# Two residual blocks in float32: the end of a layer and the start of the next, done by halves of the tokens

## The chip, the cores and the metric

The kernel runs on one core of one Trainium2 chip. The metric is the time on the device in microseconds (us), as the median of several runs; less is better. The timed runs before took 2711.64, 2714.61 and 2717.73 us.

## The reference, cut to what matters

The program computes two blocks of a network for 512 tokens of 1024 features. The first block has four layers, each of which ends in the same way, and the change touches these four ends and nothing else:

```
x = x + rms_norm(retention(rms_norm(x, g)), g_post)            # layer 1
x = x + rms_norm(conv_ffn(rms_norm(x, g)), g_post)             # layer 2
x = x + rms_norm(diff_attention(rms_norm(x, g), kv), g_post)   # layer 3
x = x + rms_norm(conv_ffn(rms_norm(x, g)), g_post)             # layer 4

def rms_norm(x, g):
    return x * rsqrt(mean(x * x over the 1024 features) + 1e-6) * g
```

The second block (a convolution layer, a sparse attention and two feed-forward layers) has no norm on a layer's output. So a layer of the first block can add nothing to `x` before the sum of the squares of all 1024 output features of a token is known, and the next layer can start nothing before `x` is there.

## The kernel before, in words

Data lies with features on the 128 partitions and tokens along the free dimension, so `x` is eight tiles of 128 features by 512 tokens (`KD` is 8, `S` is 512). A float32 product is carried by three float32r passes (`mm3`, lines 202 to 204): both operands are kept as a high and a low part, made by ScalarE (high) and VectorE (low) in `pair` (lines 213 to 217).

Weights are a stream of 128x128 tiles in chunks of eight (`Stream`). SyncE loads chunks into four raw buffers; ScalarE writes the high part (line 106) and VectorE the low part (line 107) into one of three split buffers. A chunk is split as soon as TensorE is done with the chunk three before it. While `lo_engine` is set, line 107 runs on GpSimd in VectorE's place.

A *column* is one output tile of 128 features: a bank of PSUM that collects all its products (`col`). Each finished column of a layer's output is added to the layer's sum `hs`, squared on ScalarE (line 228) and added to `post`, the running sum of squares (line 229).

The *end of a layer* is `col_halves` (line 369): the last column alone, whose last products run first for tokens 0 to 255 and then for 256 to 511, both into one bank. After each half `done` (line 282) adds it to `hs` and squares it into a tile of its own. `last_out` also sets `lo_engine` to GpSimd, and `group` takes it back after its last step.

The *start of the next* is `group` (line 326) with an update: four columns at once in a feed-forward layer (`first = 2`: two pairs of gate and value), six in the attention and in the convolution layer. The contraction is outermost: for each of the eight tiles k of `x`, `Prep.step` makes the new `x` and its two parts, and `outer` issues for every column the two products with the high part (lines 353, 354), then the one with the low part (line 357). Tile 0 goes by halves of the tokens, the others whole.

The *norm between them* sits in `residual` (line 532), at tile 0 of the group. For each half of the tokens: sums over the partitions by small matmuls (`colsum`, line 238), square root on ScalarE (line 254), a Newton step on VectorE (lines 255 and 245 to 248), and a transpose on TensorE that spreads the result over the partitions (`spread`, line 261). The update of a tile is then a product (line 549) and a product with a sum (line 550) on VectorE, and `pair` follows (lines 216, 217), then the squares for the next norm (lines 225 to 229). Sums of both halves share one bank, spread values another.

Order: the program is written in Python, and a scheduler of the framework orders the instructions of each engine by their place in the program and a model of when they become ready. The place in the trace is therefore not always that in the code. Dependencies on PSUM are kept by bank.

Below, a *seam* is such an end of a layer with the start of the next: seam 1 follows the retention, seam 2 the first feed-forward layer, seam 3 the differential attention, seam 4 the second feed-forward layer.

## Time and profile before

| | |
|---|---|
| median of three timed runs | 2714.61 us (2711.64 to 2717.73) |
| span of the profiled execution | 2714.0 us |
| TensorE busy | 2670.7 us, 98% of the span |
| VectorE busy | 1687.1 us, 62% |
| ScalarE busy | 1192.5 us, 44% |
| GpSimd busy | 174.2 us, 6% |

The page of the profile gives the span from the first to the last instruction of one execution. No time of its own is given for that execution beside its span; the span lies 0.6 us under the median of the timed runs, which themselves lie 6 us apart. Busy times are shares of the whole program; a stretch is looked at by the view of windows, which gives for any piece of the span the busy time of each engine and the clock that TensorE was granted (1.00 is 2.4 GHz, 0.50 is 1.2 GHz). Matmuls are pipelined, so the duration shown for one is longer than the distance to the next: what a matmul costs is the distance of starts.

### The profile page before, as it was taken

The numbers are of one execution on the slowest core, as the hardware profiler recorded it, in microseconds if no ns is written. First come the engines' busy times: TensorE is split into PE (matmuls) and PEld (weight loads), VectorE is DVE, ScalarE is ACT, GpSimd is POOL, SyncE is SP. The second block draws the span as 40 slices with busy tenths as digits, with TensorE's granted clock in tenths as the row PEclk, the third lists the DMA queues.
The fourth block names the chain that finished last, engine by engine and source line by source line (L and its number), as shares of the span: only waits on it lengthen the run. The fifth ranks groups of instructions, "written<-read, shape, count | busy, mean of one in ns | idle before, by whom it ended". The sixth has DMA issues, their size and how long they took to land.

```text
span 2714.0 us, 34980 instructions
## 1 busy us (share of the span) xinstructions
PE 2670.7 (98%) x13875; PEld 2217.3 (82%) x13875; DVE 1687.1 (62%) x2695; ACT 1192.5 (44%) x1936; POOL 174.2 (6%) x147
## 2 busy tenths in 40 slices
PE   9999999999999999999999999999999999999999
PEld 8888887888888877888887578888888777888887
DVE  6545558736657687755748965545547788564453
ACT  5443434434445664533434244323337676442331
POOL 0000001000012101000005300000001111000000
PEclk9999999999999999999999989999999999999999
DMA  5223222332322112232323412223343101222222
GB/s 180 81 76 101 83 74 70 101 100 94 103 78 93 55 45 73 87 100 94 103 93 101 118 62 95 100 94 118 113 141 128 36 13 39 72 98 96 96 98 86
DMA packets 73252, 243.42 MB, mean 90 GB/s; under 512 B 9216, under 2 KB 12160, under 8 KB 73088
## 3 DMA queue, kind: packets, MB, share of 16 engines
q1 hardware_dynamic: 73088, 241.18, 26.9%
q8 instruction: 109, 1.79, 0.3%
q14 instruction: 55, 0.45, 0.1%
HBM read 229.63 MB, written 4.19 MB: 86 GB/s over the span
## 4 chain that ended last, share of the span: by engine, by line
PE 88%; DVE 8%; ACT 2%; issue 1%; POOL 1%; SPq 1%; DMA 0%; POOLq 0%; ACTq 0%; DVEq 0%
PE bank L202 24%; PE bank L204 24%; PE bank L203 24%; PE bank L353 3%; PE bank L357 3%; PE bank L354 3%; DVE bank L1000 2%; PE bank L691 2%; PE bank L747 1%; PE bank L1480 1%; DVE arena_f L550 1%; PE bank L238 1%; PE bank L886 1%; DVE w_spl L107 0%; DVE arena_r L217 0%
## 5 line engine op out<-in xcount | busy, mean ns | idle before, releaser
L202 PE MATMUL bank<-arena_r,w_spl 128*128 128x512 f32 (+1 forms) x2712 | 1061.8, 392 | 3.3 <-DVE arena_f L1050 1.9
L203 PE MATMUL bank<-arena_r,w_spl 128*128 128x512 f32 (+1 forms) x2712 | 1054.5, 389 | 0.7 <-DVE arena_r L214 0.7
L204 PE MATMUL bank<-arena_r,w_spl 128*128 128x512 f32 (+1 forms) x2712 | 1051.9, 388 | 0.0
L106 ACT ACTIVATE w_spl<-w_raw 128x1024 fp32r<-128x1024 f32 (+1 forms) x424 | 448.4, 1058 | 715.8 <-PE bank L203 471.6
L107 DVE TENSOR_TENSOR w_spl<-w_raw,w_spl 128x1024 fp32r<-128x1024 f32 (+1 forms) x392 | 480.5, 1226 | 387.0 <-ACT w_spl L106 384.1
L202 PEld LDWEIGHTS bank<-arena_r,w_spl 128*128 128x128 f32 x2712 | 509.8, 188 | 108.5 <-issue 4.1
L204 PEld LDWEIGHTS bank<-arena_r,w_spl 128*128 128x128 f32 x2712 | 509.5, 188 | 105.4 <-issue 1.6
L203 PEld LDWEIGHTS bank<-arena_r,w_spl 128*128 128x128 f32 x2712 | 509.8, 188 | 101.0 <-issue 1.4
L563 DVE SCALAR_TENSOR_TENSOR arena_f<-arena_f,vec 128x510 f32<-128x510 f32 (+1 forms) x264 | 195.7, 747 | 5.5 <-ACT arena_f L561 1.8
L213 ACT ACTIVATE arena_r<-arena_f 128x512 fp32r<-128x512 f32 (+1 forms) x153 | 91.9, 610 | 191.5 <-DVE arena_f L591 153.7
L353 PE MATMUL bank<-arena_r,w_spl 128*128 128x512 f32 (+1 forms) x410 | 162.9, 399 | 10.2 <-ACT arena_r L216 8.2
L354 PE MATMUL bank<-arena_r,w_spl 128*128 128x512 f32 (+1 forms) x410 | 160.5, 393 | 0.0
L586 DVE TENSOR_TENSOR arena_f<-bank,arena_f 128x512 f32<-128x512 f32 x88 | 60.7, 689 | 131.6 <-PE bank L204 131.6
L202 PE MATMUL bank<-w_spl,arena_r 128*128 128x256 f32 (+1 forms) x480 | 138.9, 290 | 2.1 <-ACT arena_r L1267 1.6
L204 PE MATMUL bank<-w_spl,arena_r 128*128 128x256 f32 (+1 forms) x480 | 136.7, 286 | 0.1
L203 PE MATMUL bank<-w_spl,arena_r 128*128 128x256 f32 (+1 forms) x480 | 136.4, 284 | 0.0
L214 DVE TENSOR_TENSOR arena_r<-arena_f,arena_r 128x512 fp32r<-128x512 f32 (+1 forms) x153 | 100.5, 670 | 38.3 <-ACT arena_r L213 37.5
L711 ACT ACTIVATE arena_f<-bank,small 128x128 f32<-128x128 f32 (+3 forms) x192 | 99.6, 525 | 50.2 <-DVE small L708 47.0
L107 POOL TENSOR_TENSOR w_spl<-w_raw,w_spl 128x1024 fp32r<-128x1024 f32 x32 | 79.6, 2489 | 616.8 <-ACT w_spl L106 612.2
L588 ACT ACTIVATE arena_f<-arena_f 128x512 f32<-128x512 f32 x88 | 55.5, 631 | 138.7 <-DVE arena_f L563 138.6
L561 ACT ACTIVATE arena_f<-arena_f,vec 128x512 f32<-128x512 f32 x132 | 106.2, 809 | 22.5 <-DVE arena_f L582 21.5
L582 DVE TENSOR_TENSOR arena_f<-bank,arena_f 128x512 f32<-128x512 f32 x88 | 60.5, 688 | 80.3 <-PE bank L204 71.9
(225 smaller groups left out, 2928.0 us busy)
## 6 DMA issues: line engine op xcount, KB each, us to landing
w_raw<-w SPq DMA_DIRECT2D x422, 512.0 KB, 3.4
arena_f<-tab SPq DMA_DIRECT2D x10, 256.0 KB, 3.5
arena_f<-x SPq DMA_DIRECT2D x8, 256.0 KB, 7.5
x_wait<-arena_f SPq DMA_DIRECT2D x8, 256.0 KB, 2.3
arena_f<-x_wait SPq DMA_DIRECT2D x8, 256.0 KB, 2.6
out<-arena_f SPq DMA_DIRECT2D x8, 256.0 KB, 2.2
arena_r<-arena_f SPq DMA_DIRECT2D x20, 64.0 KB, 2.0
arena_r<-arena_f SPq DMA_DIRECT2D x20, 63.9 KB, 2.0
```

The source lines that it names most:

```text
L106: self.nc.scalar.activation(hi, r, AF.Copy)
L107: (self.lo_engine or self.nc.vector).tensor_tensor(lo, r, hi, op=ALU.subtract)
L202: mm(out, a[0], b[0], start=start, stop=False, skip_group_check=skip)
L203: mm(out, a[0], b[1], start=False, stop=False, skip_group_check=skip)
L204: mm(out, a[1], b[0], start=False, stop=stop, skip_group_check=skip)
L213: self.nc.scalar.activation(h, src, AF.Copy)
L214: self.nc.vector.tensor_tensor(l, src, h, op=ALU.subtract)
L353: mm(b, w[0], hi[:, sl], start=(k == 0 and sl.start == 0), stop=False, skip_group_check=True)
L354: mm(b, w[1], hi[:, sl], start=False, stop=False, skip_group_check=True)
L561: nc.scalar.activation(c.a, u.a, AF.Identity, bias=self.v(cb, j), scale=self.v(cw, 2 * nj + j))
L563: nc.vector.scalar_tensor_tensor(c.a[:, d:], u.a[:, :S - d], self.v(cw, (2 - d) * nj + j), c.a[:, d:], op0=ALU.mult, op1=ALU.add)
L711: nc.scalar.activation(p.a[:, :n], outs[c], AF.Exp, bias=mx[:, c:c + 1], accum_out=sm[:, c:c + 1])
```

## The change

The last column of a layer's output was done by halves; now the last four columns are in the retention and the attention (16 weight tiles), and the last two in the feed-forward layers (22 weight tiles). All of them run for tokens 0 to 255 first, then all for 256 to 511, each half of each column in a bank of its own (`tail`). The sums and the norm of the first half are issued inside the second half. The order on TensorE within `tail`, and within the first three tiles of the next group, is fixed as written (`in_order`). The next group does its first three tiles of `x` for the first half of the tokens, then for the second (`group_halves`); sums and spread of the second half are issued after tiles 0 and 1 of the first. Since each weight tile is used in both passes, the stream is held: no chunk is split over one that the second pass still needs (`hold`). The feed-forward layers now start with six columns instead of four (`first = 3`). The low part of the weights is always made by VectorE. Squares of tiles 0 to 2 are made later, two to a step. In the diff, comments and early exits that are also gone are left out.

```diff
@@ class Stream, take
         if o == 0:
+            h = c if self.held is None else self.held
+            assert c < h + NSPL
             self.load(c + NRAW)
-            self.parts(c + NSPL)
+            self.parts(h + NSPL)
...
+    def hold(self, chunk=None):
+        self.held = chunk
+        self.parts(((len(self.order) - 1) // CHUNK if chunk is None else chunk) + NSPL)
@@ class Prep
-    def halves(self, k):
-        return HALVES if self.update is not None and k < 1 else (slice(0, S),)
+    def half(self, k, sl):
+        b = self.b
+        if len(self.xs) == k:
+            self.xs.append((b.R.get(), b.R.get()))
+        self.update.apply(k, sl)
+        b.pair(b.x[k].a[:, sl], b.v(self.g, k), [s.a[:, sl] for s in self.xs[k]])
+        if sl.stop == S and self.want:
+            self.squares.append(k)
...
+class Residual:
+    def sums(self, i):
+        b = self.bank[i] = self.b.P.get()
+        self.b.colsum(b, self.accs, 256, True, range(2 * i, 2 * i + 2))
+    def scale(self, i):
+        self.rs[i] = self.b.rstd(self.bank[i].a[:, 256:258], 2, D)
+    def spread(self, i):
+        self.b.spread(self.bank[i], self.rs[i], 0, 2)
+    def apply(self, k, sl):
+        b, nc = self.b, self.b.nc
+        for i, half in enumerate(HALVES):
+            if half.start < sl.start or half.stop > sl.stop:
+                continue
+            h = self.hs[k].a[:, half]
+            nc.vector.tensor_tensor(h, h, self.bank[i].a[:, 0:256], op=ALU.mult)
+        x = b.x[k].a[:, sl]
+        nc.vector.scalar_tensor_tensor(x, self.hs[k].a[:, sl], b.v(self.g, k), x, op0=ALU.mult, op1=ALU.add)
...
@@ class Build, in place of last_out
+    def tail(self, name, ns, xs, ks, hs):
+        ts = {n: self.F.get() for n in ns}
+        res = Residual(self, None, hs, [self.post, ts[ns[-1]]])
...
+        def done(b, n, sl):
+            h, t = hs[n].a[:, sl], ts[n].a[:, sl]
+            nc.vector.tensor_tensor(h, h, b.a[:, sl], op=ALU.add)
+            b.free()
+            nc.scalar.activation(t, h, AF.Square)
+            if n != ns[-1]:
+                nc.vector.tensor_tensor(self.post.a[:, sl], self.post.a[:, sl], t, op=ALU.add)
...
+        with self.in_order():
+            W.held = len(W.order) // CHUNK
+            nc.scalar.activation(self.cols(1), self.eps, AF.Sqrt)
+            todo = deque([(8, lambda: res.sums(0)), (9, lambda: res.scale(0)), (20 if len(ks) > 8 else 14, lambda: res.spread(0))])
+            at = 0
+            for half, sl in enumerate(HALVES):
+                for n in ns:
+                    b = self.P.get()
+                    for i, k in enumerate(ks):
+                        if half == 0:
+                            c = len(W.order) // CHUNK
+                            ws[n, k] = c, W.take(name, k, n)
+                        else:
+                            W.hold(ws[n, k][0])
+                            at += 1
+                            while todo and at > todo[0][0]:
+                                todo.popleft()[1]()
+                        self.mm3(b.a[:, sl], ws[n, k][1], [s.a[:, sl] for s in xs[i]], i == 0, i == len(ks) - 1)
+                    done(b, n, sl)
+            W.hold()
...
+    def in_order(self):
+        return self.tc.manual_schedule(engines={mybir.EngineType.PE})
@@ group
+        if prep.update is not None:
+            first = 3
+            with self.in_order():
+                self.group_halves(name, list(ns), first, banks, prep)
+        for k in range(first, KD):
             prep.step()
...
+    def group_halves(self, name, ns, m, banks, prep):
+        W.held = len(W.order) // CHUNK
+        for half, sl in enumerate(HALVES):
+            for k in range(m):
+                prep.half(k, sl)
+                W.after = self.last_hi.ins
+                for p in range(2):
+                    for i, n in enumerate(ns):
+                        if half == 0 and p == 0:
+                            c = len(W.order) // CHUNK
+                            ws[k, n] = c, W.take(name, k, n)
+                        elif half == 1 and p == 1:
+                            W.hold(ws[k, n][0])
+                        w, b = ws[k, n][1], banks[i].a[:, sl]
+                        if p == 0:
+                            self.mm(b, w[0], xs[k][0].a[:, sl], k == 0 and half == 0)
+                            self.mm(b, w[1], xs[k][0].a[:, sl], False)
+                        else:
+                            self.mm(b, w[0], xs[k][1].a[:, sl], False)
+                if half == 0:
+                    if k == 0:
+                        res.sums(1)
+                        res.scale(1)
+                    elif k == 1:
+                        res.spread(1)
+        W.hold()
...
@@ ffn
-        first = 2 if both else 3
+        first = 3
```

## Rows read from the trace of the kernel before

**Rows 1.** The page: span and instructions; time by engine of the chain that ended last.
```profile
span 2714.0 us, 34980 instructions
PE 88%; DVE 8%; ACT 2%; issue 1%; POOL 1%; SPq 1%; DMA 0%; POOLq 0%; ACTq 0%; DVEq 0%
```

**Rows 2.** Windows, seams 1 to 4: length, busy time of each engine, clock, DMA.
```profile
core 0: us, PE busy (x) PEld busy (x) DVE busy (x) ACT busy (x) POOL busy (x), PEclk, DMA share, GB/s
413.10:451.53 38.43, 32.14 (x150) 26.43 (x149) 30.26 (x47) 16.06 (x28) 9.69 (x4) 0.87 0.19 65
786.84:830.80 43.96, 41.16 (x217) 35.38 (x215) 39.10 (x54) 22.50 (x36) 16.76 (x7) 0.96 0.24 82
1049.77:1088.99 39.22, 32.53 (x150) 26.64 (x149) 30.98 (x47) 15.95 (x28) 9.70 (x4) 0.87 0.19 64
1424.32:1468.21 43.89, 41.36 (x216) 35.33 (x215) 35.07 (x46) 17.76 (x28) 25.62 (x13) 0.96 0.21 72
```

**Rows 3.** Timeline of TensorE, seam 1: start, duration, what, [idle before, who ended it].
```profile
412.86 0.28 PE L203 MATMUL bank<-arena_r,w_spl 128*128 128x256 f32 x1
412.98 0.28 PE L204 MATMUL bank<-arena_r,w_spl 128*128 128x256 f32 x1
...
419.82 0.69 PE L261 MATMUL bank<-cst,small 128*128 128x128 f32 x2 [1.46 <-DVE small L248]
...
435.10 0.50 PE L353 MATMUL bank<-arena_r,w_spl 128*128 128x512 f32 x1 [0.72 <-ACT arena_r L216]
...
446.33 0.79 PE L353 MATMUL bank<-arena_r,w_spl 128*128 128x512 f32 x1 [2.23 <-ACT arena_r L216]
...
451.53 0.48 PE L202 MATMUL bank<-arena_r,w_spl 128*128 128x512 f32 x1
```

**Rows 4.** Timeline of TensorE, whole matmuls after seam 4: first and last of 67.
```profile
1474.89 0.39 PE L203 MATMUL bank<-arena_r,w_spl 128*128 128x512 f32 x1
...
1489.85 0.39 PE L203 MATMUL bank<-arena_r,w_spl 128*128 128x512 f32 x1
```

**Rows 5.** Timeline of all engines, seam 2: the chain from sums to the first product.
```profile
790.48 0.50 PE L238 MATMUL bank<-vec,arena_f 128*128 128x1 f32 x4
...
791.53 1.05 PE L238 MATMUL bank<-vec,arena_f 128*128 128x1 f32 x8 [0.55 <-DVE small L255]
...
791.97 0.16 DVE L248 SCALAR_TENSOR_TENSOR small<-small 128x2 f32<-128x2 f32 x1
792.44 0.41 PE L261 MATMUL bank<-cst,small 128*128 128x128 f32 x2
...
793.06 0.40 DVE L549 TENSOR_TENSOR arena_f<-arena_f,bank 128x256 f32<-128x256 f32 x1
...
793.50 0.48 DVE L550 SCALAR_TENSOR_TENSOR arena_f<-arena_f,vec 128x256 f32<-128x256 f32 x1
...
794.02 0.51 ACT L216 ACTIVATE arena_r<-arena_f,vec 128x256 fp32r<-128x256 f32 x1 [1.14 <-DVE arena_f L550]
...
794.30 0.62 PE L261 MATMUL bank<-cst,small 128*128 128x128 f32 x2 [1.45 <-DVE small L248]
...
794.58 0.58 PE L353 MATMUL bank<-arena_r,w_spl 128*128 128x256 f32 x1
```

**Rows 6.** Timeline of VectorE and GpSimd, seam 1: one operation alone and beside GpSimd.
```profile
429.44 0.74 DVE L550 SCALAR_TENSOR_TENSOR arena_f<-arena_f,vec 128x512 f32<-128x512 f32 x1
...
442.59 2.39 POOL L107 TENSOR_TENSOR w_spl<-w_raw,w_spl 128x1024 fp32r<-128x1024 f32 x1 [2.86 <-ACT w_spl L106]
442.67 2.86 DVE L550 SCALAR_TENSOR_TENSOR arena_f<-arena_f,vec 128x512 f32<-128x512 f32 x1
```

**Rows 7.** Timeline of ScalarE and VectorE, end of layer 1: the split of a chunk.
```profile
408.97 1.06 ACT L106 ACTIVATE w_spl<-w_raw 128x1024 fp32r<-128x1024 f32 x1 [1.19 <-PE bank L203]
...
410.06 1.23 DVE L107 TENSOR_TENSOR w_spl<-w_raw,w_spl 128x1024 fp32r<-128x1024 f32 x1 [0.23 <-ACT w_spl L106]
```

**Rows 8.** Timeline of TensorE in the convolution layer: a single wait.
```profile
1528.92 0.50 PE L202 MATMUL bank<-arena_r,w_spl 128*128 128x512 f32 x1 [1.93 <-DVE arena_f L1050]
```

**Rows 9.** Windows: the four microseconds behind that wait.
```profile
1529.00:1533.00 4.00, 3.83 (x18) 3.01 (x19) 4.00 (x8) 2.04 (x4) 1.45 (x2) 1.00 0.37 111
```

More of the change, by code (lines that the diff above doesn't have):

```diff
@@ L329, in group, with mm @@
         xs = prep.xs
-        K = KD
-        for k in range(K):
+        first = 0
+        if prep.update is not None:
[3 more added lines that the diff above has]
+        for k in range(first, KD):
             prep.step()
-            self.W.after = self.last_hi.ins if prep.update is not None and k < 1 else None
-            self.outer(name, ns, k, banks, xs[k], prep.halves(k))
-            if k == 7:
-                self.W.lo_engine = None
-        return banks
+            self.outer(name, ns, k, banks, xs[k])
+        while prep.squares:
+            prep.acc = self.sumsq(prep.acc, self.x[prep.squares.popleft()].a)
+        return banks
+    def group_halves(self, name, ns, m, banks, prep):
+        W, res, xs = self.W, prep.update, prep.xs
+        W.held = len(W.order) // CHUNK
+        ws = {}
+        for half, sl in enumerate(HALVES):
[22 more added lines that the diff above has]
+        W.hold()
+        W.after = None
+    def mm(self, out, a, b, start):
+        self.nc.tensor.matmul(out, a, b, start=start, stop=False, skip_group_check=True)
     def outer(self, name, ns, k, banks, xk, halves=(slice(0, S),)):
@@ L367, in col @@
         return b
-    def col_halves(self, name, n, xs, ks, done):
-        b = self.P.get()
-        ks = list(ks)
-        rest = min(len(ks), (len(self.W.order) + len(ks)) % CHUNK or CHUNK)
-        m = len(ks) - rest
-        for i in range(m):
-            self.mm3(b.a, self.W.take(name, ks[i], n), [s.a for s in xs[i]], i == 0, False, skip=True)
-        ws = [self.W.take(name, ks[i], n) for i in range(m, len(ks))]
-        for sl in HALVES:
-            for i, w in enumerate(ws, m):
-                self.mm3(b.a[:, sl], w, [s.a[:, sl] for s in xs[i]], i == 0 and sl.start == 0, i == len(ks) - 1, skip=True)
-            done(b, sl)
-        b.free()
     def retention(self):
@@ L422, in wout @@
             for n in ns:
-                if h == 3 and n == KD - 1:
-                    self.col_halves("a_out", n, fin, range(12, 16), self.last_out(out[n], True))
-                    return
+                if h == 3 and n == KD - 4:
+                    return self.tail("a_out", range(KD - 4, KD), fin, range(12, 16), out)
                 b = self.col("a_out", n, fin, range(4 * h, 4 * h + 4))
@@ L618, in ffn @@
                 for n in range(KD):
-                    if both and n == KD - 1 and j == NF - 1:
-                        self.col_halves(down, n, ps, ks, self.last_out(h_acc[n], True))
+                    if both and n == KD - 2 and j == NF - 1:
+                        res = self.tail(down, range(KD - 2, KD), ps, ks, h_acc)
                         break
@@ L928, in finish @@
                     osb[q].free()
-                for n in range(KD - (h == 7)):
+                for n in range(KD - 4 * (h == 7)):
                     late.append(woutgen(h // 4, n))
```

122 lines of the change are left out of this document (45 added, 77 removed).

## The prediction

> **What bounds the kernel now.** I read the page first: TensorE carries 88% of the chain of work that ended last, VectorE 8% [rows 1]. So outside of special places only fewer or cheaper matmuls help, and the question is where TensorE stands still or runs slowly. The list of its waits, longest first, puts nearly all of those over half a microsecond into the four seams, so I cut the trace into four windows, each from the last first-half matmul of the last column to the end of the first group's products and sums [rows 2]. The reader is to see there that TensorE counts as busy for 32 of 38 us in seams 1 and 3, and that its mean clock is 0.87 there and 0.96 in seams 2 and 4.
>
> What these windows need at full speed I take from distances of starts. A whole matmul costs (1489.85 - 1474.89)/66 = 0.2267 us [rows 4], one of half the tokens 0.12 [rows 3]. Eight records of small sums take 792.44 - 791.53 = 0.91, so 0.114 each, and two spreads 794.58 - 794.30 = 0.28 [rows 5]. By the code seam 1 has 12 + 24 half matmuls, 84 whole ones, 24 sum records and 4 spreads: 4.32 + 19.04 + 2.73 + 0.56 = 26.65 us. Seams 2 and 4 have 24 + 36 halves and 126 whole: 7.20 + 28.56 + 2.73 + 0.56 = 39.05. Against the windows the loss is 38.43 - 26.65 = 11.8, 43.96 - 39.05 = 4.9, 39.22 - 26.65 = 12.6 and 43.89 - 39.05 = 4.8, in all **34.1 us**. That is the most the change can give back, 1.3% of the span.
>
> It has three parts. The clock: 1 - 0.87 of 38.43 is 5.0 us, 5.1 in seam 3, 1.8 in each of the others, together 13.7 (the view rounds the clock, so 0.2 either way each). Waits on the norm: 0.55 and 1.46 before the sums and the spread of the second half in every seam, with little work between [rows 3, 5]. And in seams 1 and 3 waits within the group of four columns, 0.72 and 2.23 the longest [rows 3]: there VectorE is behind, since a line-550 operation that takes 0.74 us alone took 2.86 beside GpSimd's split of a chunk [rows 6].
>
> **The change part by part.**
>
> *Halves.* Two halves cost 0.24 against 0.2267, so 13.3 ns for each pair. Seams 1 and 3 go from 12 + 12 pairs (last column, tile 0 of four columns) to 48 + 54, seams 2 and 4 from 24 + 18 to 66 + 54: 78 more each, 312 x 13.3 ns = **4.2 us lost**, all on TensorE's path. The Trainium skill (TensorE: Matmul & The Clock Gate, Back-to-back issue gap) has 262 cycles for 256 columns and 518 for 512, which is 2.5 ns for a pair and by itself 0.8 us for 312, an estimate from that page. This trace does not agree: its pair costs 13.3 ns.
>
> *Waits of the norm.* Sums and Newton step of the first half now run beside the second half of the tail. From spread to first product it takes 794.58 - 792.44 = 2.14 us (spread, lines 549, 550, 216) [rows 5]. Behind the spread stand only two tiles of work, 6 x 0.12 = 0.72, and the spread itself 0.28, so 2.14 - 1.00 = **1.1 us of wait** stay at each seam. Below that it can't go, as the chain is serial; above stands what was there, 2.0 (0.55 + 1.46) [rows 3, 5]. I take 1.1. In seams 1 and 3 the tail's 16 tiles begin at a chunk's start (a split follows the end of a chunk at 408.97 [rows 7]; the last column's first half began 12 x 0.12 before 413.10 [rows 3], at 411.66, and a column is 12 x 0.2267 = 2.72, so a chunk ends with every second column). There the second chunk's first tile in the second half releases a split: 1.06 on ScalarE, 1.23 on VectorE [rows 7], at the very tile before which the sums are issued. The square root comes behind the first, the Newton step behind the second. Alone the step takes 792.44 - 790.48 = 1.96 less the 0.91 of other sums, some 1.2 from sums to spread [rows 5]; behind the split some 3.6. The six tiles between give 6 x 0.36 + 0.45 = 2.6. So **1.0 us more** in seams 1 and 3 (0 if the scheduler puts the small operations first, 2.3 if it delays the squares too). In seams 2 and 4 twelve tiles lie between, 4.3 us, and hide it.
>
> *Second half in the group.* Sums and spread of the second half lie behind the 18 half matmuls of tile 0 and of tile 1, 2.16 us each; the spread needs 1.2 and the products 2.14. That is just covered; queued on VectorE beside them are the low parts and one split of 1.23. I take **0.5 us** for each seam (0 to 2).
>
> *Group.* Whole tiles 3 to 7 with six columns give TensorE 18 x 0.2267 = 4.08 us each. VectorE was busy 30.3 us in window 1 [rows 2]; GpSimd's four splits there go, which took VectorE about 2.1 apiece where they met [rows 6], and six splits of 1.23 come: some 29 to 31 us against 34 of TensorE. So the group is bound by TensorE in all seams, and the 2.23 wait goes with its clock. For unevenness I leave **0.5 us** per seam (0 to 1.5; seams 2 and 4 had six columns before and lost little in the group).
>
> *Clock.* It fell in each seam behind 0.55 + 1.46 us of waits, and again in seam 1 behind a single 2.23 [rows 3]; behind a single 1.93 elsewhere it stayed at 1.00 [rows 8, 9]. After the change seams 2 and 4 have one wait of 1.1: no fall. Seams 1 and 3 have 1.0 and 1.1 close together: I take one fall, at the price of seam 2's, **1.8 us** each (0 to 1.8 in every seam).
>
> *Held weights.* A freed chunk needs 1.06 + 1.23 = 2.3 us [rows 7]. In seam 1 the group's first chunk is free 3.8 us into its second half; what replaces it is needed 6.48 + 4.08 = 10.6 us into it. So nothing, and 2.3 per chunk if that cover is gone. DMA issues are unchanged in number; SyncE waits for raw buffers only.
>
> Sum of what is left: seams 1 and 3 1.1 + 1.0 + 0.5 + 0.5 + 1.8 = 4.9 each, seams 2 and 4 1.1 + 0.5 + 0.5 = 2.1 each, 14.0 in all, with 4.2 for halves 18.2. Gain 34.1 - 18.2 = 15.9 us. Against the span of 2714.0, which lies 0.6 under the median, that gives **2698 us**.
>
> **The rivals.**
> *A, cleaner.* The clock stays up everywhere and the Newton step isn't late: left are 4 x 1.1 + 4.2 and a little, 10 us; 24 saved, 2690. For it: 1.93 alone cost no clock [rows 8, 9].
> *B, the waits only move.* VectorE takes the add of the tail's last half, which waits for the last matmul, ahead of lines 549 and 550 of the new group: 1.1 us more each, and the clock falls in all seams: 18.2 + 4 x 1.1 + 2 x 1.8 = 26 left, 8 saved, 2706; with two more waits of half a microsecond in the now fixed order it is within 0.2%, 2710.
> *C, slower: the held stream starves.* All three split buffers are reserved until the second pass. If every chunk of the tails and groups came late by its 2.3 us, about four to a seam, 16 x 2.3 = 37 us would go against 15.9: 2735. From seven late chunks on it is slower than before. Against it: the 10.6 us of cover above.
> *D, it doesn't bite.* The fixed order makes TensorE wait in line for sums it passed by before, and each seam loses as much as it did: 34.1 less 30 and 4.2, 2714.
>
> **How the numbers follow.** Forecast (2694 to 2704) 0.50, A 0.20, B 0.14 (nearly two thirds of it faster by over 0.2%), D 0.08, C 0.08. A change of 0.2%, 5.4 us, is about what a measurement of this kernel can tell from none. Faster: 0.50 + 0.20 + 0.09 = 0.79; same 0.05 + 0.08 = 0.13; slower 0.08. The range reaches from just below A, 2687, to behind B, 2711; C and D and a bit of B lie outside.
>
> **What would show it.** Right: in the same windows the clock at 0.95 or more in seams 1 and 3; no wait over 1.5 us; one wait of about 1.1 on ScalarE's line 216 before the first group product; no line-107 operations on GpSimd, and line 550 at 0.74 throughout; 312 more matmuls. Wrong: first products that wait 2 us or more, a clock of 0.5 behind them in all four seams, line 202 or 353's successors waiting for line 106 or 107 in the groups (C), or time lost elsewhere than in the seams.

## The result, and the profile after

The kernel after takes 2698.72 us (median of four runs, 2697.53 to 2699.84), the kernel before 2716.17 on the same chip (four runs, 2711.64 to 2718.12): ratio 0.9937, interval 0.9923 to 0.9951. The forecast was 2698 in a range of 2687 to 2711. The profiled execution after took 2698.97 us with a span of 2697.2, which is 16.8 less than the span before; the working foresaw 15.9.

The page after: span, busy times with the number of instructions of each engine, and the chain of work that ended last, by engine. (PE is TensorE, PEld its weight loads, DVE VectorE, ACT ScalarE, POOL GpSimd.)

```profile
span 2697.2 us, 35698 instructions
PE 2663.1 (99%) x14187; PEld 2223.9 (82%) x14187; DVE 1679.4 (62%) x2777; ACT 1200.1 (44%) x1956; POOL 118.8 (4%) x125
...
PE 89%; DVE 7%; ACT 2%; issue 1%; POOL 0%; DMA 0%; SPq 0%; POOLq 0%; ACTq 0%; DVEq 0%
```

The reader is to see that little moved on this level: TensorE 88 to 89% of the chain, VectorE 8 to 7% [rows 1]. The change lives in 8% of the span, so the windows have to answer. They now begin with the first half product of the tail and end with the group's last sums. Columns: length, busy time of TensorE, its weight loads, VectorE, ScalarE and GpSimd, granted clock, DMA.

```profile
403.00:454.87 51.87, 49.87 (x324) 45.93 (x322) 38.37 (x79) 23.04 (x39) 0.00 (x0) 0.97 0.27 83
769.11:823.02 53.91, 52.46 (x359) 48.72 (x358) 41.60 (x80) 27.67 (x44) 0.00 (x0) 1.00 0.28 88
1032.88:1083.18 50.30, 48.35 (x323) 44.42 (x322) 38.35 (x79) 23.07 (x39) 0.00 (x0) 1.00 0.27 84
1397.45:1452.31 54.86, 52.75 (x359) 48.65 (x358) 39.70 (x72) 23.28 (x36) 8.61 (x18) 1.00 0.28 87
```

With the prediction's durations, seams 1 and 3 hold 204 half matmuls, 90 whole ones, 24 sums and 4 spreads: 24.48 + 20.40 + 2.73 + 0.56 = 48.17 us; seams 2 and 4 have 36 halves more, 52.49. Against the windows' lengths the losses are 3.7, 1.4, 2.1 and 2.4, **9.6 us** where 34.1 were lost [rows 2]. (The windows are longer than those before, since half columns now belong to the seam.) Clocks of 0.87, 0.96, 0.87, 0.96 became 0.97, 1.00, 1.00, 1.00.

The waits that are left show in TensorE's timeline: start, duration, operation, in brackets the idle time and who ended it. Seam 1 first, then seam 3.

```profile
411.63 0.95 PE L289 MATMUL bank<-vec,arena_f 128*128 128x1 f32 x8
...
415.39 0.43 PE L312 MATMUL bank<-cst,small 128*128 128x128 f32 x2 [0.55 <-DVE small L299]
...
417.98 3.88 PE L457 MATMUL bank<-arena_r,w_spl 128*128 128x256 f32 x18 [1.45 <-ACT arena_r L267]
421.66 1.03 PE L289 MATMUL bank<-vec,arena_f 128*128 128x1 f32 x8
...
1045.22 0.43 PE L312 MATMUL bank<-cst,small 128*128 128x128 f32 x2 [0.50 <-DVE small L299]
...
1047.81 2.42 PE L457 MATMUL bank<-arena_r,w_spl 128*128 128x256 f32 x18 [1.45 <-ACT arena_r L267]
```

These stand against [rows 3, 5]. Line 289 is the sums (238 before), 312 the spread (261), 299 the end of the Newton step (248), 267 the high part (216), and 457 the first product of the group. The sums of the first half run 3.8 us ahead of the spread, inside the tail; those of the second (421.66) come without a wait. Waits of 0.72 and 2.23 within the group are gone. Seams 2 and 4 have only the 1.45, and seam 4 one of 0.67 later: just ahead of it GpSimd's own work for the convolution layer (line 1045) runs, and beside it VectorE's line 280 takes 1.49 instead of 0.68 and line 204 1.09 instead of 0.74. The losses are made of these: in seam 1 0.55 + 1.45 and 1.7 of the clock are 3.7.

Why 1.45 and not the forecast 1.1? VectorE (DVE) and ScalarE (ACT) in seam 4, from the spread at 1413.44 to the first product at 1415.98:

```profile
1413.86 0.75 DVE L202 TENSOR_TENSOR arena_f<-arena_f,bank 128x256 f32<-128x256 f32 x2
1414.57 0.42 DVE L337 TENSOR_TENSOR arena_f<-arena_f,bank 128x256 f32<-128x256 f32 x1
1414.91 0.87 DVE L204 SCALAR_TENSOR_TENSOR arena_f<-arena_f,vec 128x256 f32<-128x256 f32 x2
1415.02 0.42 ACT L339 ACTIVATE arena_f<-arena_f 128x256 f32<-128x256 f32 x1 [2.54 <-DVE arena_f L337]
1415.42 0.51 ACT L267 ACTIVATE arena_r<-arena_f,vec 128x256 fp32r<-128x256 f32 x1
```

Between the products of tiles 0 and 1 with the spread (202) and the update of tile 0 (204) stands the add of the tail's last half (337), which waits for the tail's last matmul (1414.25 + 0.28). So line 204 starts 1.05 us behind line 202, where line 550 started 0.44 behind 549 before. The square (339) stands ahead of the high part on ScalarE but costs nothing: line 267 starts 0.03 behind the end of the first update (1414.91 + 0.48), as line 216 did 0.04 behind line 550 before. From spread to product it takes 2.54 instead of 2.14 [rows 5]. This is rival B's mechanism, at a third of its price.

One loss is new, behind the group of seam 1 (and at 1102 and 1108 behind that of seam 3). TensorE:

```profile
474.00 0.50 PE L255 MATMUL bank<-arena_r,w_spl 128*128 128x512 f32 x1 [0.38 <-DVE w_spl L107]
480.20 0.50 PE L253 MATMUL bank<-arena_r,w_spl 128*128 128x512 f32 x1 [0.92 <-ACT w_spl L106]
```

VectorE ahead of the first of them:

```profile
471.40 1.41 DVE L642 SCALAR_TENSOR_TENSOR arena_f<-arena_f,vec 128x510 f32<-128x510 f32 x2
472.72 1.22 DVE L107 TENSOR_TENSOR w_spl<-w_raw,w_spl 128x1024 fp32r<-128x1024 f32 x1
```

The 30 us there, after:

```profile
470.00:500.00 30.00, 28.68 (x124) 22.82 (x123) 29.49 (x42) 16.17 (x22) 0.00 (x0) 1.00 0.35 108
```

And 30 us in the same layer before:

```profile
485.00:515.00 30.00, 30.00 (x134) 24.86 (x133) 23.34 (x31) 14.37 (x18) 0.00 (x0) 1.00 0.28 92
```

Three pairs of gate and value leave the wide group at once, and their convolution and gating (lines 642 to 670) fill VectorE (29.49 of 30 us). Splits of the weights stand in its line, and TensorE does 124 matmuls where it does 134 otherwise: 10 x 0.2267 = 2.3 us lost (2.2 by the distances of starts). That is more than the 1.3 shown as idle, as a matmul's recorded 0.39 to 0.50 is longer than its 0.2267 of cadence. The same two waits stand in e3 below (at 473 and 480), the kernel before with the wide group: they are the wide group's.

Last a correction. The section on the change says that the low part of the weights is always made by VectorE, and the prediction expected no such operation on GpSimd. GpSimd's line 107 after:

```profile
L107 POOL TENSOR_TENSOR w_spl<-w_raw,w_spl 128x1024 fp32r<-128x1024 f32 x10 | 24.0, 2402 | 34.9 <-ACT w_spl L106 34.9
```

And before:

```profile
L107 POOL TENSOR_TENSOR w_spl<-w_raw,w_spl 128x1024 fp32r<-128x1024 f32 x32 | 79.6, 2489 | 616.8 <-ACT w_spl L106 612.2 <-DVE arena_f L549 4.4
```

The ten left belong to the convolution layer, which sets `lo_engine` for itself. Only the seams' 22 moved to VectorE.

### The profile page after: what moved, and what is told of

Read it like the earlier page. It is cut to its first block, busy times and chain, and to the rows that moved or that the text cites. A ratio compares the mean times of both kernels' runs of the same rounds, so it can differ in the third digit from the quotient of the medians.

```text
span 2697.2 us, 35698 instructions
## 1 busy us (share of the span) xinstructions
PE 2663.1 (99%) x14187; PEld 2223.9 (82%) x14187; DVE 1679.4 (62%) x2777; ACT 1200.1 (44%) x1956; POOL 118.8 (4%) x125
## 4 chain that ended last, share of the span: by engine, by line
PE 89%; DVE 7%; ACT 2%; issue 1%; POOL 0%; DMA 0%; SPq 0%; POOLq 0%; ACTq 0%; DVEq 0%
PE bank L253 23%; PE bank L255 23%; PE bank L254 23%; PE bank L473 3%; PE bank L474 3%; PE bank L477 3%; PE bank L770 2%; PE bank L457 2%; DVE bank L1079 1%; PE bank L1559 1%; PE bank L826 1%; PE bank L1068 1%; PE bank L289 1%; DVE w_spl L107 1%; DVE arena_f L642 1%
## 5 line engine op out<-in xcount | busy, mean ns | idle before, releaser
L253 PE MATMUL bank<-arena_r,w_spl 128*128 128x512 f32 (+1 forms) x2732 | 1059.5, 388 | 4.8 <-ACT w_spl L106 2.6
L254 PE MATMUL bank<-arena_r,w_spl 128*128 128x512 f32 (+1 forms) x2732 | 1052.3, 385 | 0.8 <-DVE arena_r L265 0.8
L255 PE MATMUL bank<-arena_r,w_spl 128*128 128x512 f32 (+1 forms) x2732 | 1049.4, 384 | 0.8 <-DVE w_spl L107 0.8
L107 DVE TENSOR_TENSOR w_spl<-w_raw,w_spl 128x1024 fp32r<-128x1024 f32 (+1 forms) x414 | 507.3, 1226 | 401.6 <-ACT w_spl L106 398.6
L473 PE MATMUL bank<-arena_r,w_spl 128*128 128x512 f32 (+1 forms) x350 | 136.2, 391 | 2.2 <-ACT arena_r L264 1.9
L474 PE MATMUL bank<-arena_r,w_spl 128*128 128x512 f32 (+1 forms) x350 | 135.7, 389 | 0.0
L787 DVE TENSOR_REDUCE small<-bank 128x1 f32<-128x128 f32 (+3 forms) x192 | 86.6, 483 | 23.2 <-PE bank L775 22.5
```

What stands on the lines that cost most here:

```text
L107: (self.lo_engine or self.nc.vector).tensor_tensor(lo, r, hi, op=ALU.subtract)
L253: mm(out, a[0], b[0], start=start, stop=False, skip_group_check=skip)
L254: mm(out, a[0], b[1], start=False, stop=False, skip_group_check=skip)
L255: mm(out, a[1], b[0], start=False, stop=stop, skip_group_check=skip)
L473: mm(b, w[0], hi[:, sl], start=(k == 0 and sl.start == 0), stop=False, skip_group_check=True)
L474: mm(b, w[1], hi[:, sl], start=False, stop=False, skip_group_check=True)
```

## The experiments

The theory: TensorE had been standing, and its clock falling, for two separate reasons. First, small serial steps of the norm had nothing beside them (cured by halves of the tail and of the group). Second, VectorE was behind in the seams (cured by taking GpSimd's splits off its side, and by the wide group). The rival: one of the parts does it all, the rest is cost. There are three series of runs (e1 to e4, e5 to e8, e9 to e12), each with the kernel before on the same chip (medians 2713.98, 2714.70 and 2715.43 us). The ratios are to that, and they, not the medians, compare kernels of different series.

| kernel | median us | ratio (95% interval) | span |
|---|---|---|---|
| after, split on GpSimd in the seams (e1) | 2707.12 | 0.9978 (0.9969 to 0.9987) | 2702.4 |
| after, four columns in the group (e2) | 2700.97 | 0.9950 (0.9938 to 0.9963) | 2699.2 |
| before, six columns and split on VectorE (e3) | 2703.13 | 0.9964 (0.9951 to 0.9976) | 2703.4 |
| after, earlier spread (e4) | 2695.62 | 0.9935 (0.9922 to 0.9947) | 2693.8 |
| after, tail of one column (e5) | 2706.44 | 0.9970 (0.9958 to 0.9981) | 2706.3 |
| after, group of one tile by halves (e6) | 2718.56 | 1.0015 (1.0006 to 1.0024) | 2716.7 |
| e4, update ahead of splits (e7) | 2701.48 | 0.9953 (0.9940 to 0.9966) | 2699.7 |
| e7, splits ahead of gated pairs (e8) | 2696.87 | 0.9933 (0.9920 to 0.9946) | 2695.6 |
| e4, splits ahead of gated pairs (e9) | 2691.07 | 0.9912 (0.9898 to 0.9926) | 2688.0 |
| e9, tail's adds and update ahead of splits (e10) | 2688.88 | 0.9903 (0.9889 to 0.9917) | 2686.0 |
| before, split on VectorE (e11) | 2706.66 | 0.9970 (0.9959 to 0.9982) | 2704.3 |
| after once more (e12) | 2699.02 | 0.9941 (0.9922 to 0.9960) | 2697.7 |

Where the time goes is clearest from the record of TensorE's clock. In the seams of the profiled executions a granted clock of 0.50 (1.2 GHz) cost 13.7 us of full-speed work before and 1.7 after; 11.9 in e5, 10.2 in e6 and e11, 5.1 in e3, 3.4 in e2, e7 and e8, 1.7 in e12, and nothing in e1, e4, e9 and e10. So a good part of what the waits cost comes by the clock behind them. It varies from run to run of one kernel, too: e8 has 2692.90 us at a mean clock of 0.997 and 2698.80 at 0.995.

### Who splits the weights, and how wide the group is

e1 gives the seams' splits back to GpSimd in the kernel after.

```diff
@@ tail
+            W.lo_engine = nc.gpsimd
@@ group
             self.outer(name, ns, k, banks, xs[k])
+            if k == 7:
+                self.W.lo_engine = None
```

> The changed kernel, with the low part of the weights given back to GpSimd from the tail of a layer to the end of the next group, as it was before. Theory (in seams 1 and 3 VectorE held up the group because it met GpSimd's splits): six splits per group slow VectorE by about 2.1 us each and take 1.2 us each from it, so VectorE needs some 35 us where TensorE needs 34; waits of 1 to 3 us return in each group, 2703 to 2709 us, with line 204 near 2.8 us where it meets a split. Rival (TensorE has cover enough with six columns, the gain came from the norm alone): 2697 to 2700 us.

2707.12, so 8 us come back. The profiled run is the fastest of eleven (2704.17 us, mean clock 0.997) and shows 5.2 of them in its span; the others reach 2712.12 at 0.994. VectorE and GpSimd (POOL) in seam 1 of it, with TensorE's two waits:

```profile
413.21 2.38 POOL L107 TENSOR_TENSOR w_spl<-w_raw,w_spl 128x1024 fp32r<-128x1024 f32 x1 [6.33 <-ACT w_spl L106]
413.47 2.40 DVE L341 TENSOR_TENSOR arena_f<-arena_f 128x256 f32<-128x256 f32 x1 [0.91 <-ACT arena_f L339]
...
416.85 0.43 PE L312 MATMUL bank<-cst,small 128*128 128x128 f32 x2 [1.70 <-DVE small L299]
...
419.45 1.33 PE L460 MATMUL bank<-arena_r,w_spl 128*128 128x256 f32 x9 [1.45 <-ACT arena_r L267]
```

Line 341, an add from the tail's code that takes 0.42 us alone, takes 2.40 and ends as GpSimd's split ends; the Newton step behind it starts at 415.80, and the wait for the spread grows from 0.55 to 1.70. It is [rows 6] again, in another operation and at a dearer place. So the theory had the time and the collision right and the place wrong: it looked for waits of 1 to 3 us at the group's tiles, and what came is at the two spreads (1.70 and 0.43 here).

e2 narrows the group of the feed-forward layers in the kernel after.

```diff
-        first = 3
+        first = 2 if both else 3
```

> The changed kernel, with four columns instead of six at the start of the two feed-forward layers of the first block. Theory (VectorE is the limit of a narrow group): a tile then gives TensorE 12 x 0.2267 = 2.7 us and VectorE about 3.2 us, so 2 to 3 us are lost in each of seams 1 and 3, while the waits of 0.38 and 0.92 us behind those two groups go: 2700 to 2703 us. Rival (the width is indifferent since the first three tiles run by halves and VectorE gets ahead there): 2695 to 2698 us, only the waits behind the groups go.

2700.97, inside the theory's range and 2.2 us above the kernel after, but the two intervals overlap (0.9938 to 0.9963 against 0.9923 to 0.9951), and two of its five runs, 2697.68 and 2698.54, are as fast as that kernel. In the profile 1.7 of the 2.0 us between the spans are the clock: it cost 3.4 in seam 3 where the kernel after lost 1.7 in seam 1. So what the width is worth net is not shown to differ from nothing. What it trades is shown: TensorE waits 0.3 to 0.4 twice in each narrow group, and the waits of 0.38 and 0.92 behind it are gone.

e3 makes both edits in the kernel before and leaves its tail and its halves alone; e11 makes the splits alone.

```diff
@@ last_out
-        self.W.lo_engine = nc.gpsimd
@@ ffn, in the first of the two kernels only
-        first = 2 if both else 3
+        first = 3
```

> The kernel before, with six columns at the start of the feed-forward layers and the low part of the weights always on VectorE at the seams; no halves beyond those it had, and no fixed order. Theory: the waits of 0.72, 0.26 and 2.23 us and the second fall of the clock in seams 1 and 3 go, the waits of the norm (0.55 and 1.46 us) and the first fall of the clock stay: 9 to 12 us under the kernel before, so 2703 to 2707 us, and the halves bring only 5 to 8 us of the 17. Rival (the whole gain is in the waits of the norm and the clock that falls behind them): 0 to 4 us under the kernel before.

> The kernel before, with nothing changed but that the low part of the weights in the seams is made by VectorE and not by GpSimd. Theory (the split on GpSimd slowed VectorE beside it, and the price adds to that of the narrow group): the wait of 2.23 goes; the wide group alone was worth 2.2 us in the kernel after, so 2703.1 + 2.2 = 2705, all but 2 of what both edits gave together. Rival (with four columns VectorE is the bound in seams 1 and 3, and giving it the splits costs what the shared port did): 2711 to 2715.

2703.13 and 2706.66. Taking out one assignment brings 8 us (ratio 0.9970) of the change's 17; the width adds 2 (0.9964, intervals that overlap). The theory of e11 had the sum about right and left one thing out. The wait of 2.23 at tile 7 goes, but one of 1.76 comes at tile 2. ScalarE and TensorE there:

```profile
429.04 1.06 ACT L106 ACTIVATE w_spl<-w_raw 128x1024 fp32r<-128x1024 f32 x1 [4.17 <-PE bank L356]
430.76 0.50 PE L352 MATMUL bank<-arena_r,w_spl 128*128 128x512 f32 x1 [1.76 <-ACT arena_r L216]
```

ScalarE has the high part of a chunk (106) in its line ahead of that of the next tile (216), and line 106 waits until TensorE is done with the chunk whose buffer it needs. Part of what went is a fall of the clock: in windows of 2 us, the clock of seams 1 and 3 fell twice before, for 5.1 us of lost work in each, and once here, for 3.4 in each. That is 3.4 us of the 9.7 by which the spans differ; the rest is shorter waits, and 0.7 and 0.9 from seam 2 and seam 4 on.

### The columns of the tail and the tiles of the group

e5 does only the last column by halves, e6 only the first tile of the group.

```diff
@@ the first kernel, retention (attention and feed-forward layers alike)
-                if h == 3 and n == KD - 4:
-                    return self.tail("a_out", range(KD - 4, KD), fin, range(12, 16), out)
+                if h == 3 and n == KD - 1:
+                    return self.tail("a_out", range(KD - 1, KD), fin, range(12, 16), out)
@@ the second kernel, group and group_halves
-            first = 3
+            first = 1
...
-                    elif k == 1:
+                    if k == min(1, m - 1):
                         res.spread(1)
```

> The kernel after, but the tail done by halves is the last column alone in all four layers; the groups stay by halves for three tiles. Theory (the tail of several columns is there to hide sums, Newton step and spread of the first half): in seams 1 and 3 the second half of one column is only 4 tiles, 1.44 us, so the sums come behind it, then 1.2 us to the spread and 1.9 from the spread to the products, 3.1 us of wait in place of 2.0, with a fall of the clock in both (1.8 to 5 us each, where now one of them has it); in seams 2 and 4 the sums still fit, the spread doesn't, a wait of 1.9 in place of 1.45. Given back: 138 pairs of halves x 13.3 ns = 1.8 us. Sum 2 x 1.1 + 0.9 + 2 to 7 of clock - 1.8: 2701 to 2707. Rival (the halves of the group do the work, the extra columns only cost): 1.8 us less than the kernel after, 2697.

> The kernel after, but only tile 0 of the next group goes by halves, and sums and spread of the second half both stand behind tile 0's first half. Theory (three tiles are there to hide the norm of the second half): in each seam TensorE waits 1.2 us for the second spread and 1.9 for the products behind it, 3.1 us that are now hidden, and the clock falls in some (0 to 3 us a seam); 144 pairs of halves x 13.3 ns = 1.9 us are given back. 4 x 3.1 - 1.9 = 10.5 us and up to 12 of clock: 2709 to 2720. Rival (the norm of the second half is ready anyway, since the last columns are done early): 2 us less than the kernel after, 2697.

2706.44 and 2718.56: both in the theory's ranges, both rivals (2697 us) out. TensorE in seam 1 with one column, where the sums follow the tail:

```profile
415.09 0.95 PE L289 MATMUL bank<-vec,arena_f 128*128 128x1 f32 x8
417.24 0.43 PE L312 MATMUL bank<-cst,small 128*128 128x128 f32 x2 [1.21 <-DVE small L299]
419.45 3.75 PE L457 MATMUL bank<-arena_r,w_spl 128*128 128x256 f32 x18 [1.78 <-ACT arena_r L267]
```

And with one tile, the second half's sums at 420.81:

```profile
420.81 0.95 PE L289 MATMUL bank<-vec,arena_f 128*128 128x1 f32 x8
423.17 0.43 PE L312 MATMUL bank<-cst,small 128*128 128x128 f32 x2 [1.41 <-DVE small L299]
425.38 4.21 PE L457 MATMUL bank<-arena_r,w_spl 128*128 128x256 f32 x18 [1.78 <-ACT arena_r L267]
```

In both, TensorE stands 3.0 to 3.2 us for the norm of one half. With one tile it does so once more than in the kernel before, which issued the sums of the second half ahead of the first spread [rows 5]; so with the order fixed but nothing behind which to hide the second half, the change is slower than no change by 0.15% (1.0015, 1.0006 to 1.0024). The parts don't add up: from the kernel after, 8 us go with the tail's columns and 20 with the group's tiles, together more than the whole gain. Either part alone leaves the norm of one half uncovered, and the clock falls behind the waits in all four seams again.

### What is left, and a better kernel

e4 issues the first half's sums, scale and spread earlier in the tail.

```diff
-            todo = deque([(8, lambda: res.sums(0)), (9, lambda: res.scale(0)), (20 if len(ks) > 8 else 14, lambda: res.spread(0))])
+            todo = deque([(4, lambda: res.sums(0)), (4, lambda: res.scale(0)), (12 if len(ks) > 8 else 8, lambda: res.spread(0))])
```

> The changed kernel, with sums and Newton step of the first half issued four tiles earlier or more (before tile 5 of the second pass) and the spread before tile 9 (retention, attention) or tile 13 (feed-forward), so that 2.5 to 3.6 us of products stand behind it instead of 0.7. Theory (the wait of 1.45 us before the first group product is the serial chain of 2.5 us behind a spread that comes too late): the four waits of 1.45 fall to under 0.6 and the two of 0.5 in front of the spread go, no clock falls: 2690 to 2694 us. Rival (VectorE takes the adds of the tail's last half and a split first, so the chain ends when the tail ends wherever the spread stands): 2697 to 2700 us.

2695.62, between the theory and the rival. Waits of 0.50 and 0.55 are gone and 1.45 fell to 0.76, 0.41, 0.73 and 0.41, but in seams 2 and 4 one of 0.75 came at tile 1. VectorE and TensorE in seam 2 show why:

```profile
781.18 0.41 DVE L202 TENSOR_TENSOR arena_f<-arena_f,bank 128x256 f32<-128x256 f32 x1
...
781.68 1.23 DVE L107 TENSOR_TENSOR w_spl<-w_raw,w_spl 128x1024 fp32r<-128x1024 f32 x1
...
782.82 0.48 DVE L204 SCALAR_TENSOR_TENSOR arena_f<-arena_f,vec 128x256 f32<-128x256 f32 x1
...
783.22 0.74 DVE L202 TENSOR_TENSOR arena_f<-arena_f,bank 128x256 f32<-128x256 f32 x2
...
784.83 1.22 DVE L107 TENSOR_TENSOR w_spl<-w_raw,w_spl 128x1024 fp32r<-128x1024 f32 x1
...
785.97 0.87 DVE L204 SCALAR_TENSOR_TENSOR arena_f<-arena_f,vec 128x256 f32<-128x256 f32 x2
...
787.85 1.34 PE L457 MATMUL bank<-arena_r,w_spl 128*128 128x256 f32 x9 [0.75 <-ACT arena_r L267]
```

A split (107) stands between the two steps of an update (202, 204), of tile 0 and again of tile 1. e7 puts the updates ahead of the splits; e8 adds the same for the splits behind the group, ahead of the gated pairs.

```diff
@@ group_halves, both kernels
-                prep.half(k, sl)
+                with self.tc.high_priority():
+                    prep.half(k, sl)
@@ Stream.parts, the second kernel only (hot: feed-forward tiles 3 to 7)
+                with self.tc.high_priority() if self.hot else nullcontext():
                     ...
@@ ffn
         for j in range(NF):
+            self.W.hot = both and first <= j < first + 5
```

> The kernel with the early spread (sums 4, scale 4, spread 8 or 12 in the tail), and the update and pair of the group's half tiles put ahead of the weight splits in VectorE's order. Theory (what is left of the waits in the early-spread kernel, 0.75 at tile 1 in seams 2 and 4, is the two splits between the lines 202 and 204 of the new group): those two go, some 1.5 us, 2694 against 2695.6; the 0.4 to 0.76 at tile 0 shrink by the part that a split has in them, 2692 at best. Rival (the splits put back are then late themselves): the wait moves to a tile whose weights come late, 2695 to 2698.

> As the kernel before this one in the list (early spread, update ahead of splits), and the splits of the weights behind the groups of the feed-forward layers, five hidden tiles long, put ahead of the gated pairs on ScalarE and VectorE. Theory (the two waits behind the group in seams 1 and 3, 0.38 and 0.92 us, are splits queued behind the pairs of three gated tiles): they go, 2 x 1.3 = 2.6 us less than that kernel, about 2691. Rival (the pairs are then late, or the splits wait for a buffer that TensorE frees and not for the engines): no change or up to 2 us more, 2694 to 2696.

e7 failed: 2701.48, 6 us worse than e4, and for neither side's reason. By the record of the clock 5.1 of it are two falls that e4 doesn't have, 3.4 in seam 1 and 1.7 at 872 us, in the attention. The first of them stands behind this wait of TensorE in seam 1:

```profile
419.21 1.21 PE L458 MATMUL bank<-arena_r,w_spl 128*128 128x256 f32 x8 [1.30 <-DVE arena_f L337]
```

The updates passed not only splits but the last two adds of the tail (337), whose banks the group's columns wait for. e8 is 4.6 us better than e7, more than the 2.6 expected, since the waits behind the groups cost 2.2 each and not the 1.3 they show (the clock cost both the same, 3.4 in a seam and 1.7 in the attention). e9 has the second edit without the first; e10 gives the tail's adds and squares the same precedence as the updates, so that neither passes the other.

```diff
@@ tail, done
+            with self.tc.high_priority():
                 nc.vector.tensor_tensor(h, h, b.a[:, sl], op=ALU.add)
                 b.free()
                 nc.scalar.activation(t, h, AF.Square)
                 ...
```

> The kernel with the early spread, and with the weight splits behind the groups of the feed-forward layers ahead of the gated pairs; VectorE's order in the group itself is left to the scheduler. Theory (the two waits of 0.38 and 0.92 behind the groups are such splits, and no more hangs on them): 2695.6 - 2.6 to 4.1 = 2691.5 to 2693. Rival (the 4.6 us between the two kernels of the last series came from the clock, which fell in another seam): 2695 to 2696.

> As the kernel ahead, and the update and pair of the group's half tiles together with the adds and squares of the tail's columns put ahead of the weight splits on VectorE and ScalarE, so that no update passes an add of the tail. Theory (putting the updates ahead failed only because they passed the tail's last adds, on whose banks TensorE waited 1.3 us): the waits of 0.41 to 0.76 at tiles 0 and 1, 3.8 us over the four seams, go for the most part, and those 1.3 don't come: 2688 to 2691. Rival (what is put back, the splits, is late in its turn): 1.2 us per split that TensorE meets, 2693 to 2697.

2691.07 and 2688.88. The 30 us behind seam 1 in e9:

```profile
470.00:500.00 30.00, 30.00 (x134) 24.86 (x133) 29.82 (x43) 17.71 (x25) 0.00 (x0) 1.00 0.29 89
```

VectorE is as full as in the kernel after, yet TensorE does its 134 again: order was wanting there, not room. From the group's last sums in seam 1 to the first sums in seam 2 it is 322.2 us where e4 has 324.4, and 2.2 less behind seam 3. That is 4.3 of the 5.8 us between the spans, and near the 4.5 between the medians; in both the clock fell in no seam, so the rival is out. e10 differs from e8 by the precedence of the tail's adds and squares alone, and is 8.0 us faster: the adds that were passed were the fault of e7. In e10 no wait is left at the start of a group. TensorE in seam 1:

```profile
412.59 0.43 PE L314 MATMUL bank<-cst,small 128*128 128x128 f32 x2
...
421.88 0.43 PE L314 MATMUL bank<-cst,small 128*128 128x128 f32 x2 [0.66 <-DVE small L301]
```

And VectorE ahead of that second spread:

```profile
418.13 2.35 DVE L109 TENSOR_TENSOR w_spl<-w_raw,w_spl 128x1024 fp32r<-128x1024 f32 x2
420.40 0.15 DVE L308 TENSOR_SCALAR small<-bank 128x2 f32<-128x2 f32 x1
```

What is left is 0.50 to 0.66 for the spread of the second half in three seams: two splits (here line 109) now stand ahead of its Newton step (from line 308). e10 beats both kernels, at 0.9903 of the time before. No clock is lost in its seams; the 6.8 us that the clock still costs there lie in the convolution layer (from 1503 and 1540 us), which no edit here touches.

### The clock

e12 is the kernel after once more.

> The kernel after once more, unchanged. Seams 1 and 3 have the same two waits there (0.5 and 1.45 us), but the clock fell in seam 1 alone. Theory (what decides is how the waits fall in time against the chip's own beat, not the place): the fall may be in another seam, in both or in none, at the same waits. Rival (the work ahead of the seam decides): it falls in seam 1 again and in no other. The time within 1.5 us of 2698.7 in either case.

2699.02; the clock fell in seam 1 and in no other, as in the first profile. So two profiles of this kernel speak for the rival. But the size of the waits doesn't decide alone. Seams 1 and 3 of the kernel after, from 411 and from 1041:

```profile
411.00:427.00 16.00, 14.00 (x104) 13.60 (x103) 12.63 (x38) 5.73 (x13) 0.00 (x0) 0.89 0.21 68
1041.00:1057.00 16.00, 14.05 (x117) 13.64 (x116) 14.30 (x42) 7.29 (x16) 0.00 (x0) 1.00 0.20 67
```

Seam 1 of e1:

```profile
411.00:427.00 16.00, 12.41 (x102) 11.81 (x101) 13.70 (x35) 5.44 (x13) 4.77 (x2) 1.00 0.21 68
```

The same waits of 0.5 and 1.45, and once 0.89, once 1.00; in e1 waits of 1.70, 1.45 and 0.43 in 9 us, and 1.00 throughout, at least in this run.

Nor does the work ahead decide alone. The single wait of 1.93 in the convolution layer, behind which the clock stayed at 1.00 before [rows 8, 9], is in every kernel here but e3, where it is 1.66. The kernel after has it at 1513.05, and the clock behind it is another:

```profile
1513.00:1517.00 4.00, 3.79 (x12) 2.90 (x13) 4.00 (x8) 2.02 (x4) 1.46 (x1) 0.64 0.29 98
```

It fell there in the profiles of after, e1, e2, e5, e7, e9, e10 and e12, and not in those of before, e4, e6, e8 and e11, though e4 and e9, for one, have the same code there.

## Why the prediction was right

The mechanism was right: sums, norm and spread run beside the halves, VectorE keeps up in the group, most of the seams' waits go, and the clock stays up but once. The time came out 0.7 us from the forecast, and the sum of what is left, 18.2 us, agrees to the tenth: 9.6 in the seams, 4.2 for halves, 2 x 2.2 behind the groups. That is luck in part. For the seams 14.0 was forecast and 9.6 came; the 4.4 behind the groups, which no step had, happen to fill the gap. And by four runs the kernel before takes 2716.17 us: from there the forecast gain of 15.9 leads to 2700.3, and 17.4 was measured.

- *Losses before, 34.1 us, most of them recoverable.* Held: 24.5 of it went from the seams, about half of that (12.0) by the record of the clock. With 4.2 and 4.4 taken off, 15.9 of the 16.8 us between the spans are accounted for; the other 0.9 lies behind seam 4. That nearly all waits over half a microsecond lie in the seams is misread: of 30 in the trace before, 14 lie elsewhere (15.9 of 32.7 us), 1.93 and 1.94 in the convolution layer among them. No sum rests on it, but the waits elsewhere are the larger part of those that are left.
- *Halves, 4.2 us.* Held as far as the traces show: 14187 matmuls against 13875, the 312 foreseen, and the cadence of halves after is 0.12 us again. No run took the halves away with all else kept.
- *Wait at the group's start, 1.1.* Too small: 1.45 in every seam, 1.4 us in all. The step took the serial chain alone and left out that the tail's last add falls into it. e4 and e10 took nearly all of it away by an earlier spread, so it was no lower bound either; "below that it can't go" held only with the spread where the change put it.
- *Late Newton step, 1.0 in seams 1 and 3.* Right place and cause (in seam 1 VectorE has line 107 from 412.85 to 414.08, the Newton step from 414.33), half the size: 0.55 and 0.50.
- *Second half in the group, 0.5; unevenness of the group, 0.5.* Both too careful: none for the second half, and in the group only 0.67 in seam 4. e6 shows that the tiles do hide it, 3 us a seam.
- *Clock, 1.8 in seams 1 and 3.* Fell in seam 1 alone (1.7). The reasoning from two close waits to a fall isn't good for a single seam, nor is that from a single 1.93 to none: behind the same wait it fell in the kernel after.
- *Held weights, nothing.* Right in the seams; no late chunk.
- *The step that is missing.* All steps looked into the four windows. The wide group lets go three gated pairs at once, and 2.2 us were lost twice behind it, where before nothing was. e2 (narrower) and e9 (another order) each take it away. Time lost elsewhere than in the seams was one of the prediction's own signs of being wrong.
- *The other signs.* The clock (0.97 and 1.00 in seams 1 and 3), no wait over 1.5 us in the seams and the 312 matmuls came as foretold. The ten splits of the convolution layer stay on GpSimd, and the update of a whole tile (line 204, 550 before) takes 0.74 or 0.75 except twice in seam 4, 1.53 and 1.09 beside GpSimd's line 1045.
- *What the gain is from.* The prediction put VectorE's relief and the wide group beside each other without a price for each. e11 shows that nearly half of the gain (8 of 17 us) comes by taking out one line, the one that gave GpSimd the splits. The halves, most of the code, bring 4 us by the medians and 7 by the ratios beyond e3, and 14 to 17 once the spread comes earlier and VectorE's line is in order (e10).

Rival A's price came only with e9, a kernel with two more edits (2691 against 2690), by A's own two conditions: no fall of the clock in any seam and no late Newton step. B's mechanism is there at 0.4 us a seam. C and D were not seen.

## What to carry to other kernels

Where a fast engine waits, look first at what a slow engine does beside the one that it waits for: moving 22 operations off GpSimd was worth half of a far larger change. When work is overlapped by halves, both halves need cover, and whoever widens a stage should look at the queue behind it too, not only at the window that was mended. An order wish for one group of operations can let them pass more than was meant, here the adds that free TensorE's banks; give the work that must not be passed the same precedence.

## What the runs showed of the hardware

- What VectorE loses beside GpSimd goes by the length of GpSimd's operation, not by its own, so small steps of a serial chain lose most for their size. In e1 an add of 0.42 us took 2.40 beside a split of 2.38, above; a later pair, VectorE and GpSimd in its group:

```profile
420.42 2.38 POOL L107 TENSOR_TENSOR w_spl<-w_raw,w_spl 128x1024 fp32r<-128x1024 f32 x1 [4.83 <-ACT w_spl L106]
420.77 2.31 DVE L268 SCALAR_TENSOR_TENSOR arena_r<-arena_f,vec,arena_r 128x256 fp32r<-128x256 f32 x1
```

Line 268 takes 0.48 alone. Both VectorE operations end 0.28 us behind the split (415.87 and 415.59, 423.08 and 422.80). Operations on 512 columns end 0.55 behind it, wherever inside it they began: in the kernel before line 550 began 0.08 us into a split and took 2.86 [rows 6], and line 217 began 1.23 into one (431.30 and 430.07) and took 1.73. Operations with one input in PSUM were not held up. In e1, inside a split:

```profile
784.81 2.39 POOL L107 TENSOR_TENSOR w_spl<-w_raw,w_spl 128x1024 fp32r<-128x1024 f32 x1 [1.32 <-ACT w_spl L106]
786.12 0.75 DVE L202 TENSOR_TENSOR arena_f<-arena_f,bank 128x256 f32<-128x256 f32 x2 [1.86 <-PE bank L312]
```

Two of them take 0.75 there, as they do in the kernel after with GpSimd idle (1413.86, above). The Trainium skill (SBUF — State Buffer, SBUF: two separate sides) says that VectorE and GpSimd share a pair of ports that one of them locks for a whole instruction, against VectorE operations with two inputs in SBUF among others. Lines 341 and 268 have two such inputs, and the trace agrees.
- The clock fell, or didn't, at equal waits: at 0.5 and 1.45 us within 3 us once in two seams, in the same seam in two profiles; not at all behind 1.70, 1.45 and 0.43; behind a single 1.93 in eight profiles and not in five. The runs of e1 had mean clocks of 0.997 to 0.994 at 2704.17 to 2712.12 us, so it also changes from one execution of a kernel to the next. What else decides stays open. A fall cost 1.7 us of full-speed work, or two or three times as much: summed over windows of 2 us, what a seam lost to the clock was 1.70 to 1.72, 3.40 to 3.42 or 5.12 wherever it fell, in the kernels before, after and seven of the experiments (in e3 the clock is recorded at 0.95 even where nothing waits, at no cost in time, as whole matmuls keep their 0.2267 us there, and it is left out here). In time, seam 1 of the kernel after took 1.6 us longer than seam 3, whose waits are 0.05 shorter (51.87 and 50.30): the smallest fall cost about 1.5.
